# Group A's weighted sums with the queries on the partitions, and the norm taken by an accumulating square on ScalarE

## The chip, the core and the metric

The kernel runs on one core of one Trainium2 chip. A time is the device time of one execution in microseconds; the kernel before took 3307.88 us (median of three, 3305.25 to 3311.66). One further execution was profiled: it took 3308.65 us, of which 3306.8 us lie between its first and its last instruction (the span).

TensorE, called PE in the profile, multiplies a stationary tile (loaded by a weight load, PEld) with a moving tile and writes to PSUM. VectorE is DVE, ScalarE is ACT, GpSimd is POOL, SyncE is SP and issues the DMAs.

## The reference, cut to what matters

```python
def differential_attention(q, k, v, lam):          # group A: 4 heads, v has 128 columns
    for blk in range(S // QBLOCK):                 # S = 2048, chunk-causal mask
        s = jnp.einsum('bqhmd,bkhmd->bhmqk', q[:, t0:t1], k[:, :t1]) * scale
        pr = jax.nn.softmax(jnp.where(mask, s, -jnp.inf), axis=-1)
        w = pr[:, :, 0] - lam * pr[:, :, 1]        # two maps per head
        outs.append(jnp.einsum('bhqk,bkhe->bqhe', w, vf[:, :t1]))
...
oa = differential_attention(aq, ak, av, lam)
oa = rms_norm(oa, subln_g[i]) * (1.0 - lambda_init)   # x * rsqrt(mean(x^2) + eps) * g, over the 128 columns
ob = stick_breaking_attention(...)                    # group B: 8 heads
mix = jnp.concatenate([oa, ob], axis=-1)
h = layer_norm(ALPHA * h + mix @ w_out, ln1_g, ln1_b)
h = layer_norm(ALPHA * h + swiglu_ffn(h), ln2_g, ln2_b)
h = layer_norm(ALPHA * h + sigmoid(h @ w_ple_gate + b) * (p @ w_ple_proj), ln3_g, ln3_b)
```

## The kernel before, in words

All of it is float32. Where accuracy is wanted from the fast matmul, a value is split into a rounded part hi and a remainder lo (`split`, L201: ACT writes hi, DVE or POOL writes lo), and a product is three matmuls: hi by hi, hi by lo, lo by hi (`mm3`, L196). Tokens go in four groups of 512. The dense work (projection `pj`, output projection `acc<-w,mT`, feed-forward `gu` and `acc<-w,ft`) is the main stream. Beside it, `Beside` (L79) feeds in the attention work, and ties it to the dense matmuls by added dependencies; a scheduler that plays the program through then fixes the order on each engine. Every engine works through its order strictly; an instruction that waits holds up all that stand behind it on that engine.

Group A's work is done for one head and 256 queries at a time, 32 such heads-and-queries in all. For each, `scores_a` (L476) makes the scores and both softmaxes, with the queries on the partitions. `sums_a` (L526) turns the weights by transposing matmuls so that the keys lie on the partitions (tile `pt`), splits them (tile `wt`), and sums weights times values over the blocks of 128 keys into the PSUM tile `av`. In the kernel before `av` has the 128 value columns on the partitions and the 256 queries along the free axis: the value tile is stationary (hi twice, lo once) and 256 columns of `wt` move. In the last block of a head only the second 128 queries take part. ACT copies `av` to `y` and its square to `sq`.

`tail_a` (L567) is the norm. The squares have to be added over the partitions, so two matmuls with `sq` stationary against a column of ones make the sums `ss` (L571) in a PSUM bank of the pool that `pt` uses as well. DVE makes the denominator `den` (L575), POOL raises it to the power -1/2 (`rst`, L577). `rst` has the queries on the partitions, `y` has them on the free axis, so two transposes of `rst`, spread over 128 columns, make `rb` (L581), and DVE multiplies `y` by the gain column `gs2` and `rb` (L582). SP stores the result to `mix_d`. A head's scores, the sums of the head before it and the tail of the one before that are merged piece by piece (`group_a`, L431), so there is about one head's time from the end of the sums to the norm.

There are three stretches with group A in them: beside the projections of the first groups (416 to 672 us), and beside the feed-forward of the first (1005 to 1255 us) and of the second token group (1700 to 2115 us). At the end of each the last sums and the last tail have nothing of group A beside them (L454).

Of the kernel before, what the change touches and what calls it, by code (L numbers as in the profile page):

```python
# [10 lines left out]
F32 = mybir.dt.float32  # L11
F32R = mybir.dt.float32r
AF = mybir.ActivationFunctionType
ALU = mybir.AluOpType
# [16 lines left out]
RS = 2.0 ** -11  # L31
# [113 lines left out]
def trunk(tc, ctx, a, out):  # L145
    nc = tc.nc
    vec, act, pe, pool, sync = nc.vector, nc.scalar, nc.tensor, nc.gpsimd, nc.sync
# [8 lines left out]
    const = ctx.enter_context(tc.tile_pool(name="const", bufs=1))  # L156
# [9 lines left out]
    mix_d = dram.tile([KT, 128, S], F32, name="mix_d")  # L166
# [3 lines left out]
    ident = const.tile([128, 128], F32, name="ident")  # L170
# [7 lines left out]
    pool.memset(mhalf, -0.5)  # L178
    epst = const.tile([128, 1], F32, name="epst")
    pool.memset(epst, EPS)  # L180
    ones = const.tile([128, 1], F32, name="ones")
    pool.memset(ones, 1.0)
    scrap = const.tile([128, 1], F32, name="scrap")


# [2 lines left out]
    acc, gu, att, avp = (pl(n, b, space=PSUM) for n, b in (("acc", 2), ("gu", 2), ("att", 3), ("avp", 1)))  # L188
# [4 lines left out]
    def bank(p, shape, name):  # L193
        return p.tile(shape, F32, name=name, tag="bank")

    def mm3(ps, lh, ll, rh, rl, first, last):  # L196
        pe.matmul(ps, lh, rh, start=first, stop=False)  # L197
        pe.matmul(ps, lh, rl, start=False, stop=False)  # L198
        pe.matmul(ps, ll, rh, start=False, stop=last)  # L199

    def split(src, hi, lo, lo_eng=None, scale=None):  # L201

        if scale is None:
            act.activation(out=hi, in_=src, func=AF.Copy)  # L204
            (lo_eng or vec).tensor_tensor(out=lo, in0=src, in1=f(hi), op=ALU.subtract)  # L205
        else:
            act.activation(out=hi, in_=src, func=AF.Copy, scale=scale)
            (lo_eng or vec).scalar_tensor_tensor(out=lo, in0=src, scalar=scale, in1=f(hi),
                                                 op0=ALU.mult, op1=ALU.subtract)
# [219 lines left out]
    QG = 256  # L429

    def group_a(qgs, heads, st, kp, ep, e1p, wp, sp, sc, tp):  # L431

        kept = st["kept"]

        def keep(what, load):

            if qgs[-1] > 3:
                return load()
            if (qgs, what) not in kept:
                kept[qgs, what] = load()  # L440
            return kept[qgs, what]

        for h in range(*heads):
            for qg in qgs:
                box = []
                gens = [(scores_a(h, qg, box, kp, ep, e1p, sp, sc, keep), 4 * (qg * 2 + 1.5) * 128 * 2 / 2400 + 0.2)]
                if st["sums"]:
                    gens.append(st["sums"])
                if st["tail"]:
                    gens.append((tail_a(*st["tail"], sp, tp), 1.0, TAIL))  # L450
                yield from merged(*gens)
                st["tail"], st["next"] = st["next"], []
                st["sums"] = (sums_a(h, qg, box, st["next"], kp, wp, sp, tp, keep), (qg + 1) * 1.07, 0.25)
        if st["ends"]():  # L454
            yield from merged(st["sums"], (tail_a(*st["tail"], sp, tp), 1.0, TAIL))
            yield from tail_a(*st["next"], sp, tp)
            st.update(sums=None, tail=None, next=None)
# [6 lines left out]
    def value_tile(kp, h, i):  # L464
        vt = kp.tile([128, 4, 2, 128], F32R, name="vt", tag="vt", bufs=2)
        sync.dma_start(out=f(vt), in_=vA_d[128 * i:128 * i + 512, h].rearrange("(t p) s e -> p t s e", p=128))
        return vt
# [58 lines left out]
    def sums_a(h, qg, box, tail, kp, wp, sp, tp, keep):  # L526
        q0 = qg * QG
        ws, l0s = box[:2], box[2]
        av = bank(avp, [128, QG], "av")
        last = q0 // 128 + 1  # L530

        def turned(i):
            ps = bank(tp, [128, 2, QG], "pt")
            wt = wp.tile([128, 2, 2, QG], F32R, name="wt", tag="wt", bufs=2)
            for u in range(2):
                for j in range(2):
                    if i + u <= q0 // 128 + j:
                        k = i + u
                        pe.transpose(ps[:, u, 128 * j:128 * j + 128],
                                     ws[j][k // 8][:, 128 * (k % 8):128 * (k % 8) + 128], ident)  # L540
            if i + 1 < last:
                split(ps, wt[:, 0], wt[:, 1])
            else:
                split(ps[:, 0], wt[:, 0, 0], wt[:, 1, 0])
                split(ps[:, 1, 128:], wt[:, 0, 1, 128:], wt[:, 1, 1, 128:])
            return wt

        wts = [turned(0)]
        yield 0.43
        for i in range(0, last + 1, 2):  # L550
            if i % 4 == 0:
                vt = keep(("v", h, i), lambda: value_tile(kp, h, i))
            if i + 2 <= last:
                wts.append(turned(i + 2))
            wt = wts.pop(0)
            for u in range(2):
                c0 = 128 if i + u == last else 0
                mm3(av[:, c0:], vt[:, (i + u) % 4, 0], vt[:, (i + u) % 4, 1],
                    wt[:, 0, u, c0:], wt[:, 1, u, c0:], i + u == 0, i + u == last)
            yield 1.07 if i + 2 <= last else 0.64  # L560
        y = sp.tile([128, QG], F32, name="y", tag="y", bufs=2)
        act.activation(out=y, in_=av, func=AF.Copy)
        sq = sp.tile([128, QG], F32, name="sq", tag="sq", bufs=1)
        act.activation(out=sq, in_=av, func=AF.Square, scale=RS)
        tail.extend((h, q0, y, sq, l0s))

    def tail_a(h, q0, y, sq, l0s, sp, tp):  # L567

        ss = bank(tp, [128, 2], "ss")
        for t in range(2):  # L570
            pe.matmul(ss[:, t:t + 1], sq[:, 128 * t:128 * t + 128], ones, start=True, stop=True)  # L571
        le = sp.tile([128, 2], F32, name="le", tag="le", bufs=2)
        vec.scalar_tensor_tensor(out=le, in0=l0s, scalar=EPS, in1=l0s, op0=ALU.mult, op1=ALU.mult)
        den = sp.tile([128, 2], F32, name="den", tag="den", bufs=2)
        vec.scalar_tensor_tensor(out=den, in0=ss, scalar=1.0 / 128.0, in1=le, op0=ALU.mult, op1=ALU.add)  # L575
        rst = sp.tile([128, 2], F32, name="rst", tag="rst", bufs=2)
        pool.tensor_tensor(out=rst, in0=den, in1=mhalf[:, 0:2], op=ALU.pow)  # L577
        yield 0.5
        rb = bank(tp, [128, QG], "rb")
        for t in range(2):  # L580
            pe.transpose(rb[:, 128 * t:128 * t + 128], rst[:, t:t + 1].to_broadcast([128, 128]), ident)  # L581
        vec.scalar_tensor_tensor(out=y, in0=y, scalar=gs2, in1=rb, op0=ALU.mult, op1=ALU.mult)  # L582
        sync.dma_start(out=mix_d[h, :, q0:q0 + QG], in_=y)
        yield 0.4


# [336 lines left out]
    wpb, op, hpb = pl("wb", 2), pl("p_o", 4), pl("p_h", 4)  # L923
# [3 lines left out]
    gs2 = const.tile([128, 1], F32, name="gs2")  # L927
# [16 lines left out]
    hx, tk, gp, sp = pl("d_h", 4), pl("d_t", 8), pl("d_g", 4), pl("d_s", 2)  # L944
# [63 lines left out]
    fp, w1, op = pl("d_f", 4), pl("d_w1", 4), pl("d_o", 2)  # L1008
# [64 lines left out]
```

## Time and profile before

| | |
|---|---|
| median of three runs | 3307.88 us (3305.25 to 3311.66) |
| the profiled execution | 3308.65 us, span 3306.8 us |
| PE busy | 3197.3 us, 97% of the span |
| weight loads busy (beside matmuls) | 2673.4 us, 81% |
| DVE busy | 1999.3 us, 60% |
| ACT busy | 1498.5 us, 45% |
| POOL busy | 1552.5 us, 47% |
| mean granted TensorE clock | 0.987 of full |
| share of PE in the chain that ended last | 76% |

A matmul's duration in the trace is the time from its start to the modelled end of its pipeline; the next one starts earlier than that. What a matmul costs PE is therefore read from the distance between starts, not from durations. A group's row gives its count, its busy time, the mean duration of one, then the idle time of the engine before its instructions and what ended most of it. In the timeline, square brackets give the idle time before an instruction and what ended it.

### The profile page before, as it was taken

What the parts mean: (1) busy time and instruction counts of PE and PEld (TensorE: products, weight loads), DVE (VectorE), ACT (ScalarE), POOL (GpSimd) and SP (SyncE); (2) the same over time, 40 slices, a digit from 0 to 9 for tenths busy, and PEclk for the clock granted to TensorE, in tenths of its full rate; (3) what the DMA queues carried; (4) which work ended last, traced back from release to release, by engine and by line L of the source; (5) the groups of instructions that cost most, each with busy time, mean ns of one, the idle gap of its engine ahead of it and who ended that gap; (6) DMA issues with size and microseconds to landing.
All of it is one profiled execution on the core that took longest, in us unless ns stands there. A gap on an engine that the chain in (4) does not pass through costs nothing.

```text
span 3306.8 us, 47726 instructions
## 1 busy us (share of the span) xinstructions
PE 3197.3 (97%) x16256; PEld 2673.4 (81%) x16256; DVE 1999.3 (60%) x3877; ACT 1498.5 (45%) x2969; POOL 1552.5 (47%) x1315
## 2 busy tenths in 40 slices
PE   7999999999999999999999999999999999999998
PEld 5888788878887878787888888778888887788886
DVE  7632677545567666777656666676666656722227
ACT  3123655435565455634644444435555553333222
POOL 5225533445552335665543333555555555654433
PEclk9999999999999999999999999999999999999999
DMA  8877898655437655443445554644343334433321
GB/s 311 302 216 242 233 279 239 195 159 166 124 107 198 177 156 145 127 136 123 116 128 166 162 172 150 186 128 146 101 118 104 108 89 125 155 126 96 97 66 67
DMA packets 341187, 516.05 MB, mean 156 GB/s; under 512 B 31184, under 2 KB 162256, under 8 KB 340944
## 3 DMA queue, kind: packets, MB, share of 16 engines
q1 hardware_dynamic: 340944, 513.01, 51.1%
q8 instruction: 129, 2.11, 0.3%
q14 instruction: 114, 0.93, 0.1%
HBM read 424.80 MB, written 88.08 MB: 155 GB/s over the span
## 4 chain that ended last, share of the span: by engine, by line
PE 76%; DVE 9%; DMA 6%; issue 4%; POOL 2%; ACT 2%; SPq 1%; DVEq 0%; ACTq 0%; POOLq 0%
PE gu L197 8%; PE gu L199 8%; PE gu L198 8%; PE acc L199 7%; PE acc L197 7%; PE acc L198 7%; PE pj L199 4%; PE pj L197 4%; PE pj L198 4%; PE pt L644 3%; PE av L664 2%; PE av L663 2%; PE ps L617 2%; PE ps L616 2%; DVE tok L238 2%
## 5 line engine op out<-in xcount | busy, mean ns | idle before, releaser
L205 POOL TENSOR_TENSOR w<-raw,w 128x512 fp32r<-128x512 f32 x464 | 621.2, 1353 | 563.7 <-ACT w L204 548.7
L205 POOL TENSOR_TENSOR w<-w1r,w 128x512 fp32r<-128x512 f32 x352 | 467.4, 1329 | 480.2 <-ACT w L204 470.7
L197 PE MATMUL gu<-hT,w 128*128 128x512 f32 x1408 | 563.9, 400 | 9.8 <-ACT w L204 4.1
L199 PE MATMUL gu<-hT,w 128*128 128x512 f32 x1408 | 557.3, 396 | 0.4 <-POOL w L205 0.4
L198 PE MATMUL gu<-hT,w 128*128 128x512 f32 x1408 | 557.0, 396 | 0.0
L204 ACT ACTIVATE w<-raw 128x512 fp32r<-128x512 f32 x464 | 289.8, 632 | 473.5 <-PE acc L199 238.7
L631 POOL TENSOR_TENSOR be<-be,pr 128x512 f32<-128x512 f32 (+2 forms) x320 | 307.9, 963 | 367.2 <-DVE pr L627 359.1
L205 DVE TENSOR_TENSOR wt<-pt,wt 128x512 fp32r<-128x512 f32 (+2 forms) x528 | 295.0, 561 | 216.1 <-ACT wt L204 212.6
L204 ACT ACTIVATE wt<-pt 128x512 fp32r<-128x512 f32 (+2 forms) x528 | 262.1, 500 | 304.8 <-PE pt L644 150.8
L204 ACT ACTIVATE w<-w1r 128x512 fp32r<-128x512 f32 x352 | 222.0, 631 | 312.2 <-PE gu L199 189.6
L197 PEld LDWEIGHTS gu<-hT,w 128*128 128x128 f32 x1408 | 267.7, 190 | 62.8 <-DVE sg L831 4.9
L199 PEld LDWEIGHTS gu<-hT,w 128*128 128x128 f32 x1408 | 266.9, 190 | 57.8 <-POOL w L205 1.0
L198 PEld LDWEIGHTS gu<-hT,w 128*128 128x128 f32 x1408 | 267.6, 190 | 50.7
L627 DVE TENSOR_TENSOR_SCAN pr<-om,cy,ps 128x513 f32<-128x513 f32 x192 | 245.7, 1280 | 90.5 <-ACT be L140 81.6
L197 PE MATMUL acc<-w,ft 128*128 128x512 f32 x704 | 281.2, 401 | 4.5 <-ACT ft L204 4.3
L198 PE MATMUL acc<-w,ft 128*128 128x512 f32 x704 | 278.0, 396 | 1.1 <-POOL w L205 1.1
L199 PE MATMUL acc<-w,ft 128*128 128x512 f32 x704 | 277.5, 396 | 0.0
L140 ACT ACTIVATE om<-ps 128x512 f32<-128x512 f32 (+2 forms) x320 | 170.6, 533 | 131.5 <-DVE ps L619 69.0
L140 ACT ACTIVATE e<-e,mx 128x1024 f32<-128x1024 f32 (+4 forms) x192 | 171.2, 894 | 76.6 <-DVE e L500 76.5
L789 DVE TENSOR_TENSOR tok<-tok,acc 128x512 f32<-128x512 f32 x216 | 146.5, 680 | 90.5 <-PE acc L199 89.6
L140 ACT ACTIVATE be<-ps 128x512 f32<-128x512 f32 (+2 forms) x320 | 170.9, 535 | 0.6 <-PE pt L644 0.6
L644 PE MATMUL pt<-ident,be 128*128 128x128 f32 x1088 | 167.9, 275 | 3.0 <-POOL be L631 2.0
(163 smaller groups left out, 7037.8 us busy)
## 6 DMA issues: line engine op xcount, KB each, us to landing
raw<-in_w_ffn_down_dram SPq DMA_DIRECT2D x176, 256.0 KB, 3.0
w1r<-in_w_ffn_gate_dram SPq DMA_DIRECT2D x176, 256.0 KB, 2.8
w1r<-in_w_ffn_up_dram SPq DMA_DIRECT2D x176, 256.0 KB, 2.8
raw<-in_w_in_dram SPq DMA_DIRECT2D x144, 256.0 KB, 4.2
kt<-kA_d SPq DMA_DIRECT2D x136, 256.0 KB, 4.2
vt<-vA_d SPq DMA_DIRECT2D x68, 512.0 KB, 4.7
kt<-kB_d SPq DMA_DIRECT2D x80, 256.0 KB, 4.2
vt<-vB_d SPq DMA_DIRECT2D x80, 256.0 KB, 3.3
```

The costliest lines, as they stand in the source:

```text
L140: i = act.activation(func=func, **kw).ins
L197: pe.matmul(ps, lh, rh, start=first, stop=False)
L198: pe.matmul(ps, lh, rl, start=False, stop=False)
L199: pe.matmul(ps, ll, rh, start=False, stop=last)
L204: act.activation(out=hi, in_=src, func=AF.Copy)
L205: (lo_eng or vec).tensor_tensor(out=lo, in0=src, in1=f(hi), op=ALU.subtract)
L238: vec.scalar_tensor_tensor(out=dst[:, hs[j]], in0=src[:, hs[j]], scalar=rstd[:, 0:1], in1=b[j], op0=ALU.mult, op1=ALU.add)
L616: pe.matmul(ps[:, :w], qt[:, 0, 128 * t:128 * t + 128], kt[:, :w], start=True, stop=False)
L627: vec.tensor_tensor_scan(out=pr[:, w::-1], data0=rev, data1=ps[:, 0:1].to_broadcast([128, w + 1]), initial=1.0 if diag else cy[:, t:t + 1] ...
L631: pool.tensor_tensor(out=be[:, :w], in0=be[:, :w], in1=pr[:, 1:w + 1], op=ALU.mult)
L644: pe.transpose(pt[:, u, 128 * j:128 * j + 128], ws[j][:, 128 * i:128 * i + 128], ident)
L789: vec.tensor_tensor(out=s, in0=s, in1=ps, op=ALU.add)
```

## The change

`av` gets the queries on the partitions: two halves t of 128 queries, each with 256 columns. For each block and half, `wt` hi (128 keys by 128 queries) is stationary and the 256 columns of the value tile, hi and lo side by side, move (L559 in the new file); then `wt` lo is stationary and the 128 hi columns move (L560), added to the first 128 columns of the half. In the last block only the second half is done. ACT copies the 128 columns of hi by lo to `y` and DVE adds the others (L563, L564); `y` now has one buffer, and `sq` and the ones column are gone.

In the tail ACT squares each half with an accumulated row sum `ss` in SBUF (L573). `le`, `den` and `rst` are as before. DVE multiplies each half of `y` by its column of `rst` (L582, waiting for POOL), PE transposes the scaled `y` into `rb` (L586), and ACT multiplies by the gain column on its way out of PSUM into `yt` (L587), which is stored. Lines after L180 are two lower in the new file up to the changed part, and `split` and `mm3` likewise.

```diff
-        av = bank(avp, [128, QG], "av")
+        av = bank(avp, [128, 2, 256], "av")
...
             for u in range(2):
-                c0 = 128 if i + u == last else 0
-                mm3(av[:, c0:], vt[:, (i + u) % 4, 0], vt[:, (i + u) % 4, 1],
-                    wt[:, 0, u, c0:], wt[:, 1, u, c0:], i + u == 0, i + u == last)
+                v = vt[:, (i + u) % 4]
+                for t in range(1 if i + u == last else 0, 2):
+                    w = wt[:, :, u, 128 * t:128 * t + 128]
+                    pe.matmul(av[:, t], w[:, 0], v.rearrange("p s e -> p (s e)"), start=i + u == t == 0, stop=False)
+                    pe.matmul(av[:, t, 0:128], w[:, 1], v[:, 0], start=False, stop=i + u == last)
             yield 1.07 if i + 2 <= last else 0.64
-        y = sp.tile([128, QG], F32, name="y", tag="y", bufs=2)
-        act.activation(out=y, in_=av, func=AF.Copy)
-        sq = sp.tile([128, QG], F32, name="sq", tag="sq", bufs=1)
-        act.activation(out=sq, in_=av, func=AF.Square, scale=RS)
-        tail.extend((h, q0, y, sq, l0s))
+        y = sp.tile([128, 2, 128], F32, name="y", tag="y", bufs=1)
+        act.activation(out=y, in_=av[:, :, 128:], func=AF.Copy)
+        vec.tensor_tensor(out=y, in0=av[:, :, 0:128], in1=y, op=ALU.add)
+        tail.extend((h, q0, y, l0s))
...
-        ss = bank(tp, [128, 2], "ss")
+        yt = sp.tile([128, QG], F32, name="yt", tag="yt", bufs=2)
+        ss = sp.tile([128, 2], F32, name="ss", tag="ss", bufs=2)
         for t in range(2):
-            pe.matmul(ss[:, t:t + 1], sq[:, 128 * t:128 * t + 128], ones, start=True, stop=True)
+            act.activation(out=yt[:, 128 * t:128 * t + 128], in_=y[:, t], func=AF.Square, scale=RS,
+                           accum_out=ss[:, t:t + 1])
...
         pool.tensor_tensor(out=rst, in0=den, in1=mhalf[:, 0:2], op=ALU.pow)
+        for t in range(2):
+            vec.tensor_scalar(out=y[:, t], in0=y[:, t], scalar1=rst[:, t:t + 1], scalar2=None, op0=ALU.mult)
         yield 0.5
         rb = bank(tp, [128, QG], "rb")
         for t in range(2):
-            pe.transpose(rb[:, 128 * t:128 * t + 128], rst[:, t:t + 1].to_broadcast([128, 128]), ident)
-        vec.scalar_tensor_tensor(out=y, in0=y, scalar=gs2, in1=rb, op0=ALU.mult, op1=ALU.mult)
-        sync.dma_start(out=mix_d[h, :, q0:q0 + QG], in_=y)
+            pe.transpose(rb[:, 128 * t:128 * t + 128], y[:, t], ident)
+        act.activation(out=yt, in_=rb, func=AF.Copy, scale=gs2)
+        sync.dma_start(out=mix_d[h, :, q0:q0 + QG], in_=yt)
```

The scheduler makes a new order from this. Three places of it follow.

PE beside the feed-forward of the second token group, before: sums of group A (`av`) between transposes (`pt`, of weights `e_...`) and scores (`ps`).

```order
L197 MATMUL av<-wt,vt 128x256
L539 MATMUL pt<-ident,e_18043 128x128
L539 MATMUL pt<-ident,e_18046 128x128
L539 MATMUL pt<-ident,e_18043 128x128
L539 MATMUL pt<-ident,e_18046 128x128
L494 MATMUL ps<-kt,qt 128x512
L495 MATMUL ps<-kt,qt 128x512
L198 MATMUL av<-wt,vt 128x256
L199 MATMUL av<-wt,vt 128x256
L197 MATMUL av<-wt,vt 128x256
L198 MATMUL av<-wt,vt 128x256
L199 MATMUL av<-wt,vt 128x256
```

The same two blocks of the same head now, where the operands have changed places and widths of 256 and 128 alternate.

```order
L559 MATMUL av<-vt,wt 128x256
L492 MATMUL ps<-kt,qt 128x512
L493 MATMUL ps<-kt,qt 128x512
L560 MATMUL av<-vt,wt 128x128
L559 MATMUL av<-vt,wt 128x256
L560 MATMUL av<-vt,wt 128x128
L559 MATMUL av<-vt,wt 128x256
L560 MATMUL av<-vt,wt 128x128
L559 MATMUL av<-vt,wt 128x256
L560 MATMUL av<-vt,wt 128x128
```

Two blocks took six matmuls of 256 columns and take eight now, four of 256 and four of 128.

PE at the end of the first stretch, before: the last sums, the last norm, then the output projection of the first token group.

```order
L198 MATMUL av<-wt,vt 128x256
L199 MATMUL av<-wt,vt 128x256
L197 MATMUL av<-wt,vt 128x128
L198 MATMUL av<-wt,vt 128x128
L199 MATMUL av<-wt,vt 128x128
L571 MATMUL ss<-ones,sq 128x1 x2
L581 MATMUL rb<-ident,rst 128x128 x2
L197 MATMUL acc<-w,mT 128x512
L198 MATMUL acc<-w,mT 128x512
```

The end of the first stretch now.

```order
L195 MATMUL acc<-w,mT 128x512
L196 MATMUL acc<-w,mT 128x512
L197 MATMUL acc<-w,mT 128x512
L586 MATMUL rb<-ident,y 128x128
L195 MATMUL acc<-w,mT 128x512
L196 MATMUL acc<-w,mT 128x512
L197 MATMUL acc<-w,mT 128x512
L195 MATMUL acc<-w,mT 128x512
L196 MATMUL acc<-w,mT 128x512
L197 MATMUL acc<-w,mT 128x512
L195 MATMUL acc<-w,mT 128x512
L586 MATMUL rb<-ident,y 128x128
```

The last `av` stood directly ahead of `ss` and `rb`; now 25 dense matmuls stand between the last `av` and the first `rb`, and seven more between the two halves of `rb`.

DVE in the first stretch, at the fifth norm, before: from the denominator on (`hl` and `rt` belong to the projection, `e` and `ps` to the scores).

```order
L575 SCALAR_TENSOR_TENSOR den<-ss,le 128x2
L573 SCALAR_TENSOR_TENSOR le<-l0s 128x2
L500 TENSOR_SCALAR e_4215,mx<-ps 128x512
L205 TENSOR_TENSOR wt<-pt,wt 128x256
L497 TENSOR_SCALAR ps<-ps,maskB 128x64 x2
L500 TENSOR_SCALAR e_4213,mx<-ps,mx 128x128
```

The same place now.

```order
L564 TENSOR_TENSOR y<-av,y 128x256
L203 TENSOR_TENSOR wt<-pt,wt 128x512
L206 SCALAR_TENSOR_TENSOR hl<-rt_6319,hl 128x512
L578 SCALAR_TENSOR_TENSOR den<-ss,le 128x2
L576 SCALAR_TENSOR_TENSOR le<-l0s 128x2
L582 TENSOR_SCALAR y<-y,rst 128x128 x2
L498 TENSOR_SCALAR e_4235,mx<-ps 128x512
L203 TENSOR_TENSOR wt<-pt,wt 128x256
```

Two instructions behind the denominator DVE now stands before a product that needs POOL's `rst`, with the scores' minimum and the next split behind it.

## Rows read from the trace of the kernel before

**Rows 1.** The page: span, busy time of each engine, chain that ended last.
```profile
span 3306.8 us, 47726 instructions
...
PE 3197.3 (97%) x16256; PEld 2673.4 (81%) x16256; DVE 1999.3 (60%) x3877; ACT 1498.5 (45%) x2969; POOL 1552.5 (47%) x1315
...
PE 76%; DVE 9%; DMA 6%; issue 4%; POOL 2%; ACT 2%; SPq 1%; DVEq 0%; ACTq 0%; POOLq 0%
```
**Rows 2.** Busy time in group A's three stretches: length, engines, granted clock, DMA share, GB/s.
```profile
416.00:672.00 256.00, 241.13 (x1475) 212.25 (x1474) 170.45 (x537) 131.42 (x306) 96.33 (x81) 0.98 0.80 233
1005.00:1255.00 250.00, 242.42 (x1285) 204.61 (x1286) 169.15 (x437) 124.38 (x262) 79.50 (x64) 0.99 0.59 175
1700.00:2115.00 415.00, 404.06 (x2082) 338.06 (x2081) 276.93 (x619) 190.45 (x355) 151.10 (x117) 1.00 0.57 169
```
**Rows 3.** Groups of PE by form: sums of group A, norm.
```profile
L198 PE MATMUL av<-wt,vt 128*128 128x256 f32 x256 | 78.2, 305 | 1.6 <-DVE wt L205 1.5
...
L571 PE MATMUL ss<-ones,sq 128*128 128x1 f32 x128 | 16.7, 235 | 3.5 <-ACT sq L564 2.8 <-DVE e L500 0.3 <-DVE r L518 0.3
...
L581 PE MATMUL rb<-ident,rst 128*128 128x128 f32 x64 | 12.4, 275 | 1.9 <-POOL om L705 1.1 <-POOL rst L577 0.8
...
L198 PE MATMUL av<-wt,vt 128*128 128x128 f32 x32 | 8.0, 250 | 0.2
```
**Rows 4.** Timeline at 1630.5 us: matmuls of 256, 128, 128 and 512 columns.
```profile
1630.52 0.28 PE L664 MATMUL av<-wt,vt 128*128 128x256 f32 x1
...
1630.64 0.22 PE L663 MATMUL av<-wt,vt 128*128 128x128 f32 x1
1630.64 0.19 PEld L664 LDWEIGHTS av<-wt,vt 128*128 128x128 f32 x1
1630.70 0.28 PE L664 MATMUL av<-wt,vt 128*128 128x128 f32 x1
1630.75 0.19 PEld L197 LDWEIGHTS gu<-hT,w 128*128 128x128 f32 x1
1630.81 0.45 PE L197 MATMUL gu<-hT,w 128*128 128x512 f32 x1
...
1631.10 0.39 PE L198 MATMUL gu<-hT,w 128*128 128x512 f32 x1
...
1631.33 0.39 PE L199 MATMUL gu<-hT,w 128*128 128x512 f32 x1
```
**Rows 5.** Timeline at 434 us: the sums of squares on PE.
```profile
434.04 0.50 PE L571 MATMUL ss<-ones,sq 128*128 128x1 f32 x4
...
434.73 0.39 PE L495 MATMUL ps<-kt,qt 128*128 128x512 f32 x1
```
**Rows 6.** Timeline at the end of the first stretch.
```profile
671.35 0.43 PE L581 MATMUL rb<-ident,rst 128*128 128x128 f32 x2 [1.09 <-POOL om L705]
...
672.86 0.63 PE L199 MATMUL acc<-w,mT 128*128 128x512 f32 x1
...
675.42 0.63 PE L199 MATMUL acc<-w,mT 128*128 128x512 f32 x1
675.85 0.50 PE L197 MATMUL acc<-w,mT 128*128 128x512 f32 x1
```
**Rows 7.** Timeline at the fifth norm: denominator, POOL's work ahead, power.
```profile
488.66 0.14 DVE L575 SCALAR_TENSOR_TENSOR den<-ss,le 128x2 f32<-128x2 f32 x1
...
491.10 1.29 POOL L205 TENSOR_TENSOR w<-raw,w 128x512 fp32r<-128x512 f32 x1 [4.12 <-ACT w L204]
492.35 0.70 POOL L577 TENSOR_TENSOR rst<-den,mhalf 128x2 f32<-128x2 f32 x1
```
**Rows 8.** Waits of POOL from 416 to 672 us: for whom, total us, times, longest.
```profile
POOL w L205 <- ACT w L204: 86.7, 31, 10.6
```
**Rows 9.** Groups of DVE by form: group B's like addition, the norm's product.
```profile
L673 DVE TENSOR_TENSOR yb<-av,yb 64x512 f32<-64x512 f32 x32 | 21.6, 675 | 11.1 <-ACT yb L672 11.1
L582 DVE SCALAR_TENSOR_TENSOR y<-y,gs,rb 128x256 f32<-128x256 f32 x32 | 15.2, 475 | 6.7 <-PE rb L581 6.4
```

More of the change, by code (lines that the diff above doesn't have):

```diff
@@ L180, in trunk @@
     pool.memset(epst, EPS)
-    ones = const.tile([128, 1], F32, name="ones")
-    pool.memset(ones, 1.0)
     scrap = const.tile([128, 1], F32, name="scrap")
@@ L556, in sums_a, with tail_a @@
             for u in range(2):
-                c0 = 128 if i + u == last else 0
-                mm3(av[:, c0:], vt[:, (i + u) % 4, 0], vt[:, (i + u) % 4, 1],
-                    wt[:, 0, u, c0:], wt[:, 1, u, c0:], i + u == 0, i + u == last)
-            yield 1.07 if i + 2 <= last else 0.64
-        y = sp.tile([128, QG], F32, name="y", tag="y", bufs=2)
-        act.activation(out=y, in_=av, func=AF.Copy)
-        sq = sp.tile([128, QG], F32, name="sq", tag="sq", bufs=1)
-        act.activation(out=sq, in_=av, func=AF.Square, scale=RS)
-        tail.extend((h, q0, y, sq, l0s))
-    def tail_a(h, q0, y, sq, l0s, sp, tp):
-        ss = bank(tp, [128, 2], "ss")
+                v = vt[:, (i + u) % 4]
[3 more added lines that the diff above has]
+                    pe.matmul(av[:, t, 0:128], w[:, 1], v[:, 0], start=False, stop=i + u == last)
+            yield 1.07 if i + 2 <= last else 0.64
+        y = sp.tile([128, 2, 128], F32, name="y", tag="y", bufs=1)
+        act.activation(out=y, in_=av[:, :, 128:], func=AF.Copy)
+        vec.tensor_tensor(out=y, in0=av[:, :, 0:128], in1=y, op=ALU.add)
+        tail.extend((h, q0, y, l0s))
+    def tail_a(h, q0, y, l0s, sp, tp):
+        yt = sp.tile([128, QG], F32, name="yt", tag="yt", bufs=2)
+        ss = sp.tile([128, 2], F32, name="ss", tag="ss", bufs=2)
         for t in range(2):
-            pe.matmul(ss[:, t:t + 1], sq[:, 128 * t:128 * t + 128], ones, start=True, stop=True)
+            act.activation(out=yt[:, 128 * t:128 * t + 128], in_=y[:, t], func=AF.Square, scale=RS,
+                           accum_out=ss[:, t:t + 1])
         le = sp.tile([128, 2], F32, name="le", tag="le", bufs=2)
```

## The prediction

> **What bounds the kernel now.** I read four views, in this order. The page first: PE is busy 97% of the span and makes up 76% of the chain that ended last, DVE is busy 60%, ACT 45%, POOL 47% [rows 1]. The reader is to see that a microsecond more or less of PE work is, to first order, a microsecond of the kernel. Then the busy time in the three stretches in which group A runs, since only these change: 241 of 256 us, 242 of 250 and 404 of 415 on PE, at a granted clock of 0.98 to 1.00 [rows 2]. So the rule holds there too, with 15, 8 and 11 us of idle PE. DVE is busy 170, 169 and 277 us in them, two thirds. Third, the groups of PE by form, for the counts: each of the three matmul lines of group A's sums has 256 instructions of 256 columns and 32 of 128 (one row of each form is shown), which makes 256 full blocks and 32 half blocks; the sums of squares are 128 passes over 32 norms, four in each [rows 3]. Last the timeline, for what a matmul costs, since the durations overlap.
>
> **Cost of a matmul by its columns.** At full clock (the upper level, 2.4 GHz) a matmul of 512 columns costs 0.23 us (1631.10 to 1631.33) and one of 256 costs 0.12 (1630.52 to 1630.64) [rows 4]. For 128 columns the row must be read with care. The step from the first to the second is 0.06 (1630.64 to 1630.70), but this is not what it costs: the weight load of each matmul starts only when the matmul before it starts, and the loads then follow each other at 0.11 (1630.64, 1630.75), so that the deficit is paid a little later: two matmuls of 128 and one of 512 take from 1630.64 to 1631.10, 0.46 us, and less 0.23 for the 512 that leaves 0.23, or about 0.11 each [rows 4]. I take 0.11: a narrow matmul costs its successor's weight load. The lower bound is the 0.06 of the step, the upper one the 0.12 of a matmul of 256 columns.
>
> The Trainium skill, "TensorE: Matmul & The Clock Gate", section "LDWEIGHTS (loading the stationary operand)", gives columns over 1.2 in ns for a load, 107 ns for 128, and the trace agrees with 0.11 us. Its section "Back-to-back issue gap" speaks against my price: about 81 ns for a matmul of 128 columns in a stream with weight loads, and 56 ns for an isolated one; by 81 ns the sums below would cost 9.5 us more instead of 22.4, and the forecast would be 3303.
>
> **The sums of group A on PE.** A full block was three matmuls of 256 columns, 0.36 us. It becomes two of 256 and two of 128: 2 x (0.12 + 0.11) = 0.46. The columns that move are as many, 768; the weight loads go from three to four, and two of them are no longer hidden. That is +0.10 us in 256 blocks, +25.6. A half block was three of 128, 0.33, and becomes one of 256 and one of 128, 0.23: -0.10 in 32 blocks, -3.2. Together +22.4 us.
>
> **The sums of squares.** Four passes and one matmul of 512 columns take from 434.04 to 434.73, 0.69 us [rows 5]; less 0.23 that leaves 0.46 per norm, in 32 norms 14.7 us that go from PE. The two transposes of each norm stay, now of `y` instead of `rst`, and cost the same. PE's work thus grows by 22.4 - 14.7 = +7.7 us.
>
> **Idle time of PE that goes.** PE waits 3.5 us for the squares before `ss` [rows 3]; ACT makes them now for itself. At the end of the first stretch it waits 1.1 us more before `rb` [rows 6], because nothing of the dense work stands between the last sums and the norm. In the new order 25 dense matmuls stand there, 25 x 0.23 = 5.8 us; the path from the last sums to `rb` grows (a copy, an addition, two squares, the power, two products instead of two ACT passes, two PE passes and the power), but hardly to that length. After this idle time the matmuls step at 0.43 us from 672.86 to 675.85 [rows 6], the lower clock level of 1.2 GHz: seven steps in 2.99 us instead of 1.61, so 1.4 us come back with it. Sum -6.0 us. The 0.8 us before other `rb` [rows 3] I leave.
>
> **What the added waits cost.** DVE's product with `rst` is new, and it waits for POOL. In the order it stands one to ten instructions behind the denominator, at the fifth norm directly behind `le`. In the trace of before that norm's denominator was done at 488.80 and `rst` at 493.05, because POOL stood for 4.1 us before a weight split [rows 7]; until now only PE's `rb` felt this, and it stood later in its queue. With the product DVE would stand there some 4 us, with a minimum of the scores and a split of `wt` behind it, for which PE waits. How often: POOL waits for such weights 31 times in the first stretch, 86.7 of 256 us, longest 10.6 [rows 8]. A third of 16 norms meets one; at about 4 us each that is some 20 us of a standing DVE. In the other two stretches I expect little of it. The addition for `y` waits for ACT's copy as group B's does (11.1 us in 32), while DVE no longer waits for `rb` (6.4 us) [rows 9]; these about cancel. No row shows what a standing DVE costs PE. The bounds: nothing, since DVE idles 86 us of this stretch already; and all 20 us, since PE's next split is behind it. Now PE idles 15 us where DVE idles 86, a sixth; a wait that falls in the middle of DVE's queue hurts more than one at an empty queue, so I take 0.3 of it, +6 us.
>
> **Work that is hidden.** ACT gets a copy, a second square and two reads of an accumulator more per norm; it idles 125 of 256 us in the densest stretch [rows 2], and the next sums do not need them. If that cover were gone, the splits of `wt` behind them would come late. DVE's additions (like one of 475 ns [rows 9]) are about balanced by the product that ACT takes over. POOL does the same work. The stores are the same. The one buffer of `y` is free in time, since `rb` of a norm stands ahead of the last sums of the next head in PE's order.
>
> **The sum.** Profiled execution 3308.65 + 7.7 - 6.0 + 6.0 = 3316.4 us. The profiled execution lies 0.8 us above the median of the runs, within their spread, so I leave it: 3316, 0.25% slower. About 0.2% (6.6 us, to 3301.3 and 3314.5) is what a measurement of this kernel can tell from no change.
>
> **The rivals.**
>
> A: narrow matmuls hide their loads, and a matmul of 128 columns costs the step of 0.06. Then a full block takes 2 x (0.12 + 0.06) = 0.36 as before and a half block 0.18 as before; the +22.4 falls away and the kernel is faster, 3294. For it speaks the step in the trace; against it that the matmul two places on starts late by as much [rows 4]. The change makes narrow matmuls alternate with wide ones, which the trace has not in a long run; the load behind each narrow one has only that one to hide behind. 0.07. (The page's 81 ns lies between A and the forecast.)
>
> B: PE's work alone decides. DVE's waits fit into its idle time, and the price is 3308.65 + 7.7 - 6.0 = 3310: no change that can be told. For it speaks DVE's idle third; against it that the product stands so near its denominator. 0.25.
>
> C: the coupling of DVE to POOL decides. All 20 us reach PE, and the longer waits drop the clock, five times 1.4 us: 3308.65 + 7.7 - 6.0 + 20 + 7 = 3337. It decides from the point where DVE, busy 170 of 256 us in the first stretch, has no reserve left ahead of PE. For it speak POOL's long waits [rows 8], against it that PE is given dense matmuls between the dependent ones. 0.20.
>
> That the change moves no work on PE as it says is not open: the orders show eight matmuls for six and no `ss`.
>
> **How the numbers follow.** Forecast 0.48, with its own range 3310 to 3324; A 0.07, B 0.25, C 0.20. The range of 3303 to 3333 leaves out A and the upper half of C. Slower by over 0.2%: three quarters of the forecast and C, 0.57. Within: the rest of the forecast, nearly all of B, 0.34. Faster: A and a little of B, 0.09.
>
> **What would show it.** Right: starts of group A's sums 0.12 and 0.11 apart in turn, no steps of 0.06 in the mean; PE busy up by about 8 us; the first stretch ends without idle PE; DVE's waits for `rst` in the first stretch, some 20 us, and a few microseconds of PE idle behind `wt` there. Wrong: four matmuls of a block in 0.36 us (A), hardly a wait of DVE for POOL (B), or PE idle up by 20 us or more with new stretches at the lower clock (C). What could upset all of it is the new order itself, which moves other work too, by a few microseconds either way.

## The result, and the profile after

The changed kernel takes 3329.2 us (median of 3324.0 to 3332.8) against 3307.3 us of the kernel before on the same chip, a ratio of 1.0065 (95% interval 1.0053 to 1.0077). Slower by 21.8 us, where 8 were forecast: the direction and the range (3303 to 3333) were right, the size was not. The profiled execution took 3324.0 us, the low end of its runs, 15.4 us more than the profiled one before; the accounts below are of that pair. It was granted a clock of 0.989, the other three runs 0.984, 0.986 and 0.988.

First the page of the changed kernel, the lines that answer to [rows 1]:
```profile
span 3322.3 us, 48041 instructions
...
PE 3196.8 (96%) x16352; PEld 2676.5 (81%) x16352; DVE 2014.8 (61%) x3941; ACT 1521.0 (46%) x3097; POOL 1558.5 (47%) x1314
...
PE 76%; DVE 10%; DMA 6%; issue 2%; ACT 2%; POOL 2%; SPq 1%; DVEq 0%; ACTq 0%; POOLq 0%
```
PE is as long busy as before, 3196.8 for 3197.3 us; the 8 us more that the prediction named as a sign are not there. So all that the span grew by, 15.5 us, is PE standing still: span less busy time rose from 109.5 to 125.5 us. PE's busy time hides two changes of opposite sign, though. The mean granted clock rose from 0.987 to 0.989, worth 6.8 us (half of the time at the lower level that is no longer there), and about as much remains that is neither wait nor clock. (Both traces issue 10,752 dense matmuls, all but 32 of them at the same place in the order, so the two can be lined up at each of them. At the last one the changed kernel is 15.4 us late: 16.0 of PE's waits, -6.8 of the clock, and 6.3 that remain.) The remainder is PE's work, but also every stall too short to show as a wait. It is good to some 5 us only: lined up with the kernel before in the same way, four kernels of the experiments below whose matmuls are those of the changed one (e2, e9, f1, f3) keep -2.7, -0.2, -3.0 and 0.5 us, and three whose matmuls are those of before (e3, e4, f4) 5.4, 1.4 and -0.4.

Where the 15.4 us come from is read in the same way at the ends of the stretches: -6.5 us at the end of the first stretch, +11 over the second, +12 over the third and its end, about -1 elsewhere. The first stretch is a gain, and the other two are the loss. In part that was in the forecast: by its prices the work alone makes -2.6, +3.5 and +6.7 us in the three, which have 64, 80 and 112 full blocks and 16, 8 and 8 norms. The waits of PE make +1.4 from 416 to 680 us, +5.7 from 1000 to 1290 and +6.0 from 1690 to 2140; of waits the forecast expected little in the last two.

What the new matmuls cost is in the timeline; here PE at 1063 us in the changed kernel (start, duration, engine, line, operation, tiles, shapes):
```profile
1063.65 0.28 PE L559 MATMUL av<-vt,wt 128*128 128x256 f32 x1
1063.77 0.22 PE L560 MATMUL av<-vt,wt 128*128 128x128 f32 x1
1063.82 0.34 PE L559 MATMUL av<-vt,wt 128*128 128x256 f32 x1
1064.00 0.22 PE L560 MATMUL av<-vt,wt 128*128 128x128 f32 x1
1064.06 0.33 PE L559 MATMUL av<-vt,wt 128*128 128x256 f32 x1
1064.22 0.22 PE L560 MATMUL av<-vt,wt 128*128 128x128 f32 x1
1064.28 0.45 PE L492 MATMUL ps<-kt,qt 128*128 128x512 f32 x1
1064.57 0.39 PE L493 MATMUL ps<-kt,qt 128*128 128x512 f32 x1
```
From the first narrow pair to the second matmul of 512 columns it is 0.92 us; less 0.23 for one such matmul that leaves 0.69 for three pairs, 0.23 each. The wide one now steps on after 0.17 and the narrow one after 0.06: it is the narrow matmul's short step that looks cheap, and the next wide one pays. The price 0.12 + 0.11 stands; over the 386 such pairs in a row at full clock in this trace the median is 0.23. The single steps of 0.12 and 0.11 that the prediction named as its sign are not there.

Then the waits of PE for the heads' own instructions, in the kernel before and in the changed one (engine, tile, line, released by; us in total, times, longest):
```profile
PE pt L539 <- DVE e L522: 5.7, 5, 3.3
...
PE ss L571 <- ACT sq L564: 2.8, 3, 1.7
...
PE rb L581 <- POOL om L705: 1.1, 1, 1.1
...
PE pt L539 <- DVE e L500: 1.0, 2, 0.8
...
PE rb L581 <- POOL rst L577: 0.8, 3, 0.3
```
```profile
PE pt L538 <- DVE e L520: 13.1, 10, 3.4
...
PE pt L538 <- DVE e L498: 2.5, 3, 1.7
...
PE rb L586 <- DVE y L582: 1.6, 3, 0.8
```
The waits for the squares and before `rb` went, 5.3 us with two of 0.3 before `ss`. In their place PE waits at `pt`, the transposes of the next head's weights, for VectorE's minimum and above all for its subtraction of the two maps: 15.6 us instead of 6.7. The new `rb` has waits of 1.6, and 7.6 us more are waits of the output projection, which had none in the kernel before. The longest of those stands directly ahead of the last `rb` of the first stretch, where dense matmuls have been put:
```profile
659.58 0.50 PE L195 MATMUL acc<-w,mT 128*128 128x512 f32 x1 [2.64 <-ACT w L202]
659.91 0.27 PE L586 MATMUL rb<-ident,y 128*128 128x128 f32 x1
```
The projection starts earlier than before and now waits for the split of its weights; at 674.79 us it waits 1.50 more for POOL's part.

Back to the waits at `pt`. The longest of these is at 1231 us; VectorE's queue there, and PE:
```profile
1226.67 3.57 DVE L520 SCALAR_TENSOR_TENSOR e<-e,r,e 128x1024 f32<-128x1024 f32 x2
1230.16 0.74 DVE L498 TENSOR_SCALAR_CACHE_REDUCE e<-ps,mx 128x512 f32<-128x512 f32 x1
1230.83 0.08 DVE L498 DVE_READ_ACCUMULATOR e<-ps,mx 128x1 f32 x1
1230.83 0.41 DVE L564 TENSOR_TENSOR y<-av,y 128x256 f32<-128x256 f32 x1
1231.17 0.67 DVE L794 TENSOR_TENSOR tok<-tok,acc 128x512 f32<-128x512 f32 x1
1232.92 0.16 DVE L509 TENSOR_TENSOR l<-l 128x1 f32<-128x1 f32 x1 [1.08 <-ACT e L140]
...
1233.37 1.95 DVE L520 SCALAR_TENSOR_TENSOR e<-e,r,e 128x1024 f32<-128x1024 f32 x2
```
```profile
1230.96 0.33 PE L538 MATMUL pt<-ident,e 128*128 128x128 f32 x1 [1.68 <-DVE e L498]
1234.71 1.54 PE L538 MATMUL pt<-ident,e 128*128 128x128 f32 x6 [3.42 <-DVE e L520]
```
PE has reached the transposes, and the minimum (1230.16), the exponentials and the second subtraction (1233.37) are still to come one behind the other. The new addition (L564) stands among them, but it delays nothing here: behind it VectorE idles 1.08 us until ScalarE's exponential is there. Nor is most of this wait new. The kernel before has it at the same place:
```profile
1231.87 1.67 PE L539 MATMUL pt<-ident,e 128*128 128x128 f32 x9 [3.31 <-DVE e L522]
```
New are waits such as the one at 2088 us, where the kernel before has none. Here the addition does stand in the way:
```profile
2086.07 0.15 DVE L517 TENSOR_SCALAR l0s<-l 128x1 f32<-128x1 f32 x1
2086.57 0.42 DVE L564 TENSOR_TENSOR y<-av,y 128x256 f32<-128x256 f32 x1 [0.35 <-ACT y L563]
2086.91 3.51 DVE L520 SCALAR_TENSOR_TENSOR e<-e,r,e 128x1024 f32<-128x1024 f32 x2
```
```profile
2088.24 1.20 PE L538 MATMUL pt<-ident,e 128*128 128x128 f32 x9 [1.75 <-DVE e L520]
```
VectorE waits 0.35 us for ScalarE's copy, adds, and starts the subtraction some 0.7 us later than it could have; PE waits 1.75 us for it.

And the wait of which the forecast made most, VectorE's for POOL's power, in the first stretch of the changed kernel:
```profile
DVE y L564 <- ACT y L563: 6.7, 5, 3.0
...
DVE y L582 <- POOL rst L580: 2.9, 5, 0.8
```
2.9 us where some 20 were expected.

### The profile page after: what moved, and what is told of

It is laid out like the page before. It is cut to its first block, busy times and chain, and to the rows that moved or that the text cites. A ratio compares the mean times of both kernels' runs of the same rounds, so it can differ in the third digit from the quotient of the medians.

```text
span 3322.3 us, 48041 instructions
## 1 busy us (share of the span) xinstructions
PE 3196.8 (96%) x16352; PEld 2676.5 (81%) x16352; DVE 2014.8 (61%) x3941; ACT 1521.0 (46%) x3097; POOL 1558.5 (47%) x1314
## 4 chain that ended last, share of the span: by engine, by line
PE 76%; DVE 10%; DMA 6%; issue 2%; ACT 2%; POOL 2%; SPq 1%; DVEq 0%; ACTq 0%; POOLq 0%
PE gu L195 8%; PE gu L197 8%; PE gu L196 8%; PE acc L197 7%; PE acc L195 7%; PE acc L196 7%; PE pj L197 4%; PE pj L195 4%; PE pj L196 4%; PE pt L649 3%; PE av L559 2%; PE av L669 2%; PE av L668 2%; DVE tok L236 2%; PE ps L621 2%
```

## The experiments

"Waits" is the sum of all of PE's waits (the rows of the view added up), and "pt for e" the two of these shown above. One head with 256 queries is called a half head from here on; VectorE's lag is the mean time from the last score matmul of a half head to the end of its last subtraction, over the 16 half heads of the second and third stretches. Ratios are against the kernel before on the same chip.

| kernel | ratio (95%) | waits, us | pt for e, us | lag, us |
|---|---|---|---|---|
| before | 1 | 97.6 | 6.7 | 10.87 |
| after | 1.0065 (1.0053 to 1.0077) | 113.4 | 15.6 | 10.99 |
| e1_wide | 1.0086 (1.0068 to 1.0104) | 115.0 | 15.5 | 10.91 |
| e2_act_product | 1.0059 (1.0039 to 1.0079) | 111.3 | 16.2 | 11.16 |
| e3_before_dve | 1.0023 (1.0011 to 1.0035) | 98.1 | 10.0 | 10.93 |
| e4_null | 1.0031 (1.0020 to 1.0043) | 93.9 | 8.2 | 10.06 |
| e5_before_no_ss | 0.9977 (0.9965 to 0.9988) | 97.2 | 12.3 | 10.66 |
| e6_ss_rounded | 1.0013 (1.0003 to 1.0024) | 103.4 | 8.5 | 10.82 |
| e7_after_ss | 1.0112 (1.0091 to 1.0133) | 108.6 | 10.5 | 11.23 |
| e9_after_null | 1.0068 (1.0049 to 1.0086) | 115.3 | 15.2 | 11.16 |
| f1_after_no_norm | 1.0058 (1.0041 to 1.0075) | 114.1 | 15.9 | 10.99 |
| f3_dve_squares | 1.0081 (1.0064 to 1.0098) | 115.8 | 17.1 | 11.15 |
| f4_before_chain | 1.0069 (1.0053 to 1.0086) | 105.7 | 7.3 | 10.97 |
| g_turned_sums_old_tail | 1.0076 (1.0063 to 1.0089) | 94.6 | 3.7 | 10.74 |

**The price of a narrow matmul.** e1_wide gives the second matmul of a pair all 256 columns:
```
-                    pe.matmul(av[:, t, 0:128], w[:, 1], v[:, 0], start=False, stop=i + u == last)
+                    pe.matmul(av[:, t], w[:, 1], v.rearrange("p s e -> p (s e)"), start=False, stop=i + u == last)
```


> The changed kernel with the narrow second matmul of each block widened from 128 to 256 moving columns (lo by both hi and lo, so no step of 128 columns is left in the sums). If a narrow matmul costs its successor's weight load, 0.11 us, widening to 0.12 costs 544 x 0.01 = 5 us at most: about 3329 to 3335 us. If a narrow matmul costs the 0.06 us of its step, widening costs 544 x 0.06 = 33 us: about 3362 us.

The ratio rose from 1.0065 to 1.0086, 7 us with intervals that meet, so near the small value and far from the large one: doubling the columns costs next to nothing, and the narrow matmul had paid for its weight load already.

**Is it VectorE's product, and its wait for POOL?** e2_act_product takes the product with `rst` to ScalarE:
```
-            vec.tensor_scalar(out=y[:, t], in0=y[:, t], scalar1=rst[:, t:t + 1], scalar2=None, op0=ALU.mult)
+            act.activation(out=y[:, t], in_=y[:, t], func=AF.Copy, scale=rst[:, t:t + 1])
```


> The changed kernel with the product of y and rst on ScalarE (64 activations with a column scale) instead of VectorE; nothing else. Theory V (the extra VectorE work in front of the subtraction that the transposes wait for is what costs, beyond the matmuls): the idle time of PE before the transposes falls from 15.6 us to about 8, the time from 3329 to about 3318 us. Theory O (the scheduler's new order costs it, not any one operation): idle time moves to other places, 3324 to 3333 us. Theory W (VectorE waiting for GpSimd's power, as predicted): the wait is gone, 3329 - 6 = 3323 us, with the change in the first stretch.

VectorE waits for POOL's power no more, and PE's waits hardly change: 111.3 and 16.2 us, where theory V expected a fall to about 8. The coupling that the forecast charged with 6 us, and rival C with 20, is not what costs.

**Is it more work on VectorE?** e3_before_dve puts such work into the kernel before:
```
+        vec.tensor_tensor(out=av, in0=av, in1=y, op=ALU.add)
...
+            vec.tensor_scalar(out=yh[:, t], in0=yh[:, t], scalar1=rst[:, t:t + 1], scalar2=None, op0=ALU.mult)
```


> The kernel before with the two VectorE steps of the changed one added and nothing taken away: an addition of y to the PSUM tile of the sums (128x256), and in the norm two products of y with the power's column (128x128 each, waiting for GpSimd). The output of group A is scaled twice by that. PE's work is unchanged. Theory V: idle time of PE before the transposes rises from 7 us to about 14, the time from 3307 to about 3317 us. If PE's own work is all that counts: 3307 us.

`pt` waits 3.3 us more for `e`, other waits less, the sum stays: 98.1 for 97.6 us. The work alone brings a ratio of 1.0023, 7.6 us; the waits of the profiled execution do not show where they go.

**How much does order alone move?** e4_null and e9_after_null declare another cost for one step of the sums to the merge, before and after; all instructions stay:
```
-            yield 1.07 if i + 2 <= last else 0.64
+            yield 1.10 if i + 2 <= last else 0.64
```


> The kernel before with one planning number changed (the cost that a block of sums tells to the merging is 1.10 instead of 1.07): the same instructions in a slightly other order. It shows how much a new order alone moves the time. Theory O: 5 us or more in either direction. Theories V and W: within 3 us, 3304 to 3310 us.

> The changed kernel with 1.10 in place of 1.07 as the cost that one step of its sums declares to the merge: the same instructions in another order. Theory S: the waits of pt for e come from what is in the tail, so they stay at 11 to 15 us and the time at a ratio of 1.0065. Theory O: the order decides, so the waits move by several us and the time by up to 0.003 (as the same edit moved the kernel before), 1.0035 to 1.0095.

Before, the new order costs 0.3%, through the clock (mean 0.985; the waits fell to 93.9 us). After, it changes nothing: 115.3 and 15.2 us. So a single order can be worth 10 us, and the waits of the changed kernel are no luck of one order. The order of the kernel before may be a lucky one: e3, e4 and f4, with the same matmuls, are all slower than it, so part of the 21.8 us may be its luck.

**Did the passes of `ss` keep the transposes back?** e5_before_no_ss leaves them out of the kernel before, e7_after_ss puts them into the changed one:
```
-        ss = bank(tp, [128, 2], "ss")
-        for t in range(2):
-            pe.matmul(ss[:, t:t + 1], sq[:, 128 * t:128 * t + 128], ones, start=True, stop=True)
+        ss = sq[:, 0:2]
```
```
+        sd = bank(tp, [128, 2], "sd")
+        for t in range(2):
+            pe.matmul(sd[:, t:t + 1], y[:, t], ones, start=True, stop=True)
```


> The kernel before without its two passes per tail over the squares; the scale of group A's result is taken from two columns of the squares instead, so its values are not the reference's. By their price 32 x 0.46 = 14.7 us of TensorE's work go. Theory S (the passes kept the first transpose of a half head apart from the next eleven, and without them the transposes come before VectorE's subtraction is done): the waits of pt for e grow from 5.7 us to about 13, other idle time likewise, and the time stays near that of the kernel before, ratio 0.999 to 1.002. Theory O (any edit gives the scheduler another order, and the waits of this one are its luck): waits of pt for e of 6 to 8 us, and nearly the whole price as a gain, ratio 0.9955, give or take the 0.003 that order alone was seen to move.

> The changed kernel with two full-precision passes per tail of y against a column of ones, at the place where the kernel before had its sums of squares; nothing reads what they write. They cost 32 x 0.46 = 14.7 us of TensorE's work. Theory S: they part the transposes again, the waits of pt for e fall from 13.1 us to 8 or less and PE's idle time by some 11, so that little is left: ratio to the kernel before about 1.0076. Theory O: the waits stay near 13 us and the passes add their price: ratio 1.011.

Neither theory fits whole. PE's waits at `pt` in e5_before_no_ss, and in e7_after_ss with those at the new passes:
```profile
PE pt L539 <- DVE e L522: 9.8, 8, 3.4
...
PE pt L539 <- DVE e L500: 2.5, 4, 1.2
```
```profile
PE pt L540 <- DVE e L522: 9.7, 7, 3.3
PE sd L572 <- DVE y L566: 3.4, 5, 0.9
...
PE sd L572 <- DVE e L500: 1.7, 3, 0.9
```
Without the passes the waits at `pt` grow by 5.6 us, with them they shrink by 5.1; the theory had the place right. But the sum of the waits follows only in part: in the kernel before it stays (97.2 for 97.6), in the changed one it falls by 4.8, for PE now waits at `sd`. A wait before a pass on the queue is no cost of the pass: take the pass away, and the next instruction waits. By its times theory O is nearer for e7 (1.0112 for 1.011). e5 gains 0.23% in the timed runs, half of the price of its passes. Lined up at the last dense matmul its profiled execution is 14.4 us early, with a remainder of -16.8; but the profile of before is from a session in which that kernel took 3307.3 us, and beside e5 it took 3300.8. Ten timed runs and one profile thus put the passes at 8 to 17 us, on both sides of their price of 14.7.

e6_ss_rounded halves the passes by rounding the squares and the ones:
```
-        sq = sp.tile([128, QG], F32, name="sq", tag="sq", bufs=1)
+        sq = sp.tile([128, QG], F32R, name="sq", tag="sq", bufs=1)
...
```


> The kernel before with its squares rounded, so that the two passes per tail are single ones (0.11 us each instead of 0.23): 32 x 0.23 = 7 us of TensorE's work go, and the passes stay where they were. Theory S: the waits stay near 5.7 us, ratio 0.998. Theory O: the mean is the same, but the order moves it by up to 0.003 either way, 0.995 to 1.001. If it is under 1 it beats both kernels.

In the profiled execution 8.7 us of the remainder went and 5.6 us of waits came, and over the runs nothing is gained: 1.0013. No version in this study that computes the reference beats the kernel before.

**Is it the squares on ScalarE, or the norm at all?** Three kernels: f1, the changed one without its norm (between the addition and the transposes nothing is left); f3, the changed one with its squares on VectorE (the first edit here); and f4, the kernel before with the changed one's chain of engines ahead of `ss` (the second):
```
-            act.activation(out=yt[:, 128 * t:128 * t + 128], in_=y[:, t], func=AF.Square, scale=RS,
-                           accum_out=ss[:, t:t + 1])
+            vec.scalar_tensor_tensor(out=yt[:, 128 * t:128 * t + 128], in0=y[:, t], scalar=RS * RS, in1=y[:, t],
+                                     op0=ALU.mult, op1=ALU.mult, accum_out=ss[:, t:t + 1])
```
```
-        act.activation(out=sq, in_=av, func=AF.Square, scale=RS)
+        vec.tensor_tensor(out=sq, in0=av, in1=y, op=ALU.add)
...
+        for t in range(2):
+            hs = sq[:, 128 * t:128 * t + 128]
+            act.activation(out=hs, in_=hs, func=AF.Square, scale=RS / 2, accum_out=s2[:, t:t + 1])
```


> The changed kernel without its norm: the squares, le, den, the power and the two products of a tail are left out, so group A's heads leave unnormalised; the sums, the addition, the transposes at the end and their copy stay. Five kernels with the sums of before had TensorE idle for 94 to 103 us, five with the sums of after for 109 to 115. Theory T (ScalarE's squares stand in its queue until VectorE has added, 15 to 27 us in all, and hold up the exponentials and splits behind them, which makes VectorE's subtraction late for the transposes): idle near 100 us, ratio 1.0025. Theory U (the turned sums and the transposes at the end do it, whatever lies between): idle stays at 109 to 115 us, ratio 1.0065.

> The changed kernel with its squares on VectorE, right behind the addition there, so that ScalarE waits for no addition; VectorE gets 64 more instructions of 128x128. Theory T: ScalarE's wait for y (15.6 us) is gone, TensorE idles for about 100 us, ratio 1.0025. Theory U: idle 109 to 115 us, ratio 1.0065.

> The kernel before with the changed kernel's chain of engines in its tail and nothing else of it: VectorE adds the two readings of the sums, and ScalarE squares the doubled result in two halves with accumulation and half the scale, so that the values are those of the reference. TensorE's instructions are those of before. Theory T: ScalarE stands for 15 us or more behind the addition, and TensorE's idle time rises from 94 to 103 us to some 110, ratio 1.004. Theory U: idle stays at 94 to 103 us, ratio 1.000 to 1.003.

Theory T falls: with the squares on VectorE and with no norm at all ScalarE waits for no addition, and PE waits as much as in the changed kernel (115.8 and 114.1 us). f4 is slower by 0.69%, but not through `pt`, though VectorE has the addition there too; PE waits before `ss`, and the clock is lower (0.985):
```profile
PE ss L575 <- ACT sq L572: 7.2, 7, 1.6
PE pt L539 <- DVE e L522: 7.1, 8, 2.6
```

**The sums or the tail?** g_turned_sums_old_tail has the sums of the changed kernel and everything behind them from the one before:
```
-        av = bank(avp, [128, QG], "av")
+        av = bank(avp, [128, 2, 256], "av")
...
-        act.activation(out=y, in_=av, func=AF.Copy)
+        act.activation(out=y, in_=av[:, :, 128:], func=AF.Copy)
-        act.activation(out=sq, in_=av, func=AF.Square, scale=RS)
+        act.activation(out=sq, in_=av[:, :, 0:128], func=AF.Square, scale=RS)
```


> The turned sums of the changed kernel with the tail of the kernel before word for word (copy and squares on ScalarE straight from the sums, two passes over the squares, rb before the product); the parts of the sums are not added and rows stand for columns, so group A's result is not the reference's. TensorE's work is that of the kernel before plus 22.4 us by the prices of 0.46 and 0.36 us. Theory U1 (the turned sums alone bring the idle time): TensorE idles for 109 to 115 us, ratio 1.011, as the changed kernel with two passes added. Theory U2 (the addition on VectorE and the transposes at the end bring it): idle 94 to 103 us as in the kernels with this tail, ratio 1.007.

This parts the change in two. The page of g:
```profile
span 3324.4 us, 48167 instructions
...
PE 3217.4 (97%) x16480; PEld 2691.6 (81%) x16480; DVE 2001.1 (60%) x3877; ACT 1498.4 (45%) x2969; POOL 1553.8 (47%) x1315
```
and its waits:
```profile
PE ss L574 <- ACT sq L567: 4.4, 4, 2.8
...
PE pt L540 <- DVE e L522: 3.1, 6, 0.9
```
The turned sums bring no waits: 94.6 us, fewer than before. Lined up at the last dense matmul, they leave a remainder of 23.5 us (17.5 late; -2.5 of waits, -3.4 of the clock), where the price said 22.4; the timed runs, 0.76% or 25 us slower, agree. Hence the waits belong to the tail: the six kernels with the old tail (e3 with its additions and e5 without its passes among them) wait for 93.9 to 103.4 us, the seven with the new one for 108.6 to 115.8, f4 with half of it for 105.7. These are single profiles, and the gap from 103.4 to 108.6 is hardly wider than what an order moved in e4 (3.7 us).

## Why the prediction was right in its direction, and where its size came from

- Work of the sums, +22.4: right. g measures 23.5; the mean of g and e7 less that of before, e3, e4 and f4 is 22.8. The Trainium skill, "TensorE: Matmul & The Clock Gate", section "Back-to-back issue gap", has about 81 ns for a matmul of 128 columns in a stream with loads; by that figure the sums would have cost an estimated 9.5 us, and the trace disagrees: in pairs with a wide matmul it is 0.11 us. Rival A is out.
- Work of the passes, -14.7: not settled. The profiled e5 has -16.8, its timed runs -7.6. After against g it is 6.3 less 23.5, -17.2, but with the mean of after, e2, e9, f1 and f3 (0.2) against that of g and e7 (24.4) it is -24. Together the profiled pair has +6.3 for the +7.7 forecast; that they are so near is luck, for the five kernels with the changed one's matmuls less the four with those of before make -1.4 in the mean. That PE's work grew is thus not shown.
- Idle time that goes, -6.0: half right. At the end of the first stretch the 1.1 us before `rb` are gone, and so is the lower clock behind it (0.66 granted from 672 to 677 us before, 1.00 now), worth 1.7 us. But the dense matmuls put there wait 2.6 and 1.5 us for their weights, which the forecast left out, so the stretch does not end without idle PE. Of the 6.5 us gained, 3.5 are a lower clock ahead of it that nobody had forecast (0.89 from 640 to 672 us before, 1.00 now). The 3.5 us before `ss`, of which 2.8 were for the squares, were no gain: e5 shows that without the passes PE meets the same lateness at `pt`.
- VectorE's wait for POOL, +6 in the first stretch: the step that failed. The wait is 2.9 us there, and e2, which takes it away, changes nothing that can be told. The mis-sized term is that of the waits as a whole, -6.0 + 6.0 = 0 in the forecast (1.4 of the 6.0 that go being clock) and +16.0 in the trace, 11.7 of them in the second and third stretches, of which the prediction said that it expected little. That the time still fell into the range is luck in this part: the waits that were priced hardly came, and others came in their place. Their source is the new tail; the norm, the engine of the squares and that of the product are ruled out as the source (f1, f3, e2). The one buffer of `y` shows no wait either: in the changed kernel ScalarE's copy into it waits for the sums alone (11.9 us). What is left of the tail is the addition on VectorE, the transposes of `y` behind it and ScalarE's copy on the way out.
- Of the addition the lag gives a hint. "About balanced by the product that ACT takes over" counted VectorE's busy time, but the addition stands elsewhere in the queue: all nine kernels with it end the last subtraction 10.91 to 11.23 us after the last scores, the five without at 10.06 to 10.87; the means, 11.05 and 10.63, differ by 0.42 us, and one addition takes 0.41. (Without e4, whose lag is the shortest, the difference is 0.28, and e3 has the lag without the waits.) And the waits at `pt` add up: 6.7 before, 3.3 more with VectorE's work alone (e3), 5.6 more without `ss` alone (e5), 15.6 with both. But f4, with the addition on VectorE and the passes, has only 0.6 more than before. That is a reading of single profiles, and it covers 9 of the 16 us; 7.6 more are the output projection's. Why other waits did not fall in exchange, as they did in e3 and e5, stays open; no run took the addition or the transposes at the end out of the new tail alone, so which of them makes PE wait is not shown.
- The profiled pair differs by 15.4 us, the medians by 21.8: the profiled execution of after is its quickest. The accounts explain the pair only, and in its clock the pair is not typical. In the sessions of the experiments the runs of before have mean granted clocks of 0.988 to 0.989, those of e2, e9, f1 and f3 of 0.985 to 0.987. A run of length t at a mean clock c loses about (1 - c) x t; by this estimate 5 to 11 of the 19 to 27 us by which these four are slower are clock, where the pair has a gain of 6.8. Why their clock is lower stays open.

## What to carry to other kernels

Price a turned product by its weight loads as well as its columns: where a narrow stationary pass replaces a wide one, the next load pays, and a step in the timeline looks cheaper than it is. A wait before an instruction that you remove is a gain only if the next one in the queue is not waiting for the same late engine; look whose lateness it is. An instruction that changes its engine takes a new place in a queue, and busy time that balances says nothing of what stands behind it there; whether that is what cost here is not shown. And line up several kernels with the same work before a remainder is called work: here such kernels differed by 9 us.

## What was not expected of the hardware

VectorE's new product, 128x128 from SBUF to SBUF, takes 0.27 to 0.29 us (once 0.23), but 10 of 64 took 0.53 to 1.39. All ten overlapped an instruction of POOL, of the 54 others four. The worst pair, on VectorE and on POOL:
```profile
2094.76 2.56 DVE L582 TENSOR_SCALAR y<-y,rst 128x128 f32<-128x128 f32 x2
```
```profile
2094.69 1.27 POOL L203 TENSOR_TENSOR w<-w1r,w 128x512 fp32r<-128x512 f32 x1
2095.93 1.29 POOL L203 TENSOR_TENSOR mT<-mraw,mT 128x512 fp32r<-128x512 f32 x1
```
Each product ends 0.1 us after POOL's split. The Trainium skill, "SBUF — State Buffer", section "Who interferes with whom", says that such an instruction of VectorE can need the port pair that it shares with GpSimd, and that whoever comes second stands until the other is done; the trace agrees, 1.3 us for 0.28. It cost little here (e2).

The denominator, whose `ss` now lies in SBUF instead of PSUM, is held up too: five of its 32 took 0.48 to 1.25 us, all five beside an instruction of POOL, while none took over 0.16 in the kernel before and in g. One of them stands directly ahead of a subtraction for which PE then waits 2.03 us:
```profile
1995.18 1.25 DVE L578 SCALAR_TENSOR_TENSOR den<-ss,le 128x2 f32<-128x2 f32 x1
1996.35 2.47 DVE L520 SCALAR_TENSOR_TENSOR e<-e,r,e 128x1024 f32<-128x1024 f32 x2
```
It is not the source of the waits as a whole: f1 has no denominator, and PE waits as much.

The other surprise is how far an order alone reaches: 0.3% by one declared cost in e4, mostly through the granted clock (half-speed time within the span: 84 us before, 98 in e4, 70 in the changed kernel).
